# Window stores on POOL's queue, memory's values beside the last scan step, w_co sums behind each cross-attention head

## The chip, the cores and the metric

The kernel runs on one core of a Trainium2 chip. The metric is the device time of one execution in microseconds; a smaller number is better. Matrix products run on PE (TensorE), whose weight loads the profile lists as PEld; elementwise work runs on DVE (VectorE), ACT (ScalarE) and POOL (GpSimd); SP (SyncE) issues nearly all DMAs. Each engine works through its own queue in order.

## The reference, cut to what matters

One layer of a hybrid encoder trunk, on x of 1024 tokens by 1024 channels and a memory of 256 tokens, all in float32:

```python
h = rms_norm(x, g_mix_pre)
aq, ak, av, dqkv, dgate, dalpha, dbeta = split(h @ w_in)
attn_o = window_attention(rope(aq), rope(ak), av, sink)      # 8 heads of 64, 2 key groups, +-128 tokens
dn_o = gated_deltanet(dqkv, dgate, dalpha, dbeta, ...)       # 4 heads of 128, both directions
x = x + rms_norm(concat(attn_o, dn_o) @ w_out, g_mix_post)
q = rms_norm(x, g_cross_pre) @ w_cq                          # 4 heads of 256
k, v = split(rms_norm(mem, g_mem) @ w_ckv)
x = x + rms_norm((softmax(q @ k.T / 16) @ v) @ w_co, g_cross_post)
g, u = split(rms_norm(x, g_ffn_pre) @ w_gate_up)             # 2 x 2816
x = x + rms_norm((silu(g) * u) @ w_down, g_ffn_post)
```

## The kernel before, in words

A float32 product is made of three products of high and low parts. `split` (l.100) casts a tile to its high part on ACT (l.103) and subtracts that from the tile on DVE, or on POOL where `eng` says so (l.104); `load_w` loads a block of weights (`wraw`, l.125) and splits it into `whi` and `wlo`.

The stages follow each other in time as follows, by the times of the profile. Until 355 us: input projection, the preparation of the delta rule and the first windows of attention. From 355 to about 520 us: the scans of the delta rule. Up to 545 us: what is left of the windows and of memory's projection. Then the output projection w_out (`mid_gemm`, PE tile `pmg`), from about 640 us cross-attention, then w_co, the feed-forward's first matrix, and from about 1295 us w_down.

The order in which the stage of the scans is written comes from a table, `ORDER_3` (l.39); `issue` calls one function for each entry. `s01` is one step of the two scans (each has two heads and both directions), interleaved in four pieces; a step loads `kv` and `pz` of the next chunk (l.859, l.860), multiplies them into the PSUM tile `psc` (l.844) and, in the last steps, forms the output `ol`, which PE transposes (l.936) and SP stores (l.941). `W` is `next_windows`: two windows of local attention, of 16 in all (2 groups of 8). `K` is `next_keys`: one block of 128 columns of memory's keys, 24 products of 128x256 into `pck` (l.984). `V` is `next_values`: half of memory's values, 48 products of 128x512 into `pcv` (l.1000). `M` is memory's norm. A scheduler with a model of the engines then arranges the instructions of each engine by their priority, which follows the order of writing. `tc.high_priority(AHEAD)` moves a block forward by 300 places, and `tc.issue_after(ins)` keeps a block behind an instruction.

A window (`window`, l.663) splits the scaled queries into `qs` (ACT, and POOL at l.677), makes four `psw` score tiles (l.685), takes their maxima with `m` (DVE, l.687), exponentials (ACT), scales them by the reciprocal `es` (l.697 to 703; l.703 on DVE for some windows, on ACT for others), transposes them (`ptw`, l.711), splits them to `ph` and `pl` and multiplies with the values into `pow` (l.716). ACT's copy and DVE's addition (l.719, l.720) put the result in `ao`, a tile with one buffer, which is stored to `d_mix` in DRAM. Once all windows and scans of a half of the tokens are there, SP loads `d_mix` back as `mraw` (l.1147) in four quarters, which are split to `s0h` and `s0l` for w_out.

`cross_attention` (l.1182) runs four heads for one half of the tokens, then four for the other: scores `pcs`, softmax `cpr`, its transposes `pct` and their split `cph`, `cpl`, and the products `pco`. Between the two halves stands the code that forms sums of blocks of w_co for a block product with fewer multiplications: four chunks, each with four loads `wpart` and, on DVE, four subtractions (l.1269 to 1274) and four splits. In w_down the PSUM banks `pdX` are added to `za` on DVE (`zv`, l.1775).

The lines of the changed kernel behind l.720 have numbers smaller by one, up to cross-attention.

Of the kernel before, what the change touches and what calls it, by code (L numbers as in the profile page):

```python
# [14 lines left out]
ALU = mybir.AluOpType  # L15
# [8 lines left out]
NT = S // P  # L24
# [4 lines left out]
AHEAD = 300  # L29
# [6 lines left out]

ORDER_1 = ("k0 k1 E0 K0 U0 E1 K1 U1 S0 q0 v0 q1 C0 v1 E2 C1 k2 E3 k3 q2 K2 U2 v2 K3 U3 S1 q3 C2 v3 C3 B0 B1").split()
ORDER_2 = "L0 L1 A4 V A0 A1 G0 G1 L2 L3 W W W A2 A3 G2 G3 W".split()
ORDER_3 = ("M " + "s01 W K " * 5 + "s01 V " + "s01 K " * 2 + "s01 K V").split()


_NAMES = ["ident", "mUi", "mLi", "m5", "m6", "band0", "band1", "band2", "mU", "mL", "ones"]
# [34 lines left out]
def tile_hybrid_block(  # L77
# [6 lines left out]
    nc = tc.nc  # L84
# [15 lines left out]
    def split(hi, lo, src, scale=None, eng=None):  # L100

        if scale is None:
            nc.scalar.copy(hi, src)  # L103
            return (eng or nc.vector).tensor_tensor(lo, src, f32(hi), ALU.subtract)  # L104
        nc.scalar.activation(hi, src, AF.Identity, scale=scale)
        return nc.vector.scalar_tensor_tensor(lo, src, scale, f32(hi), ALU.mult, ALU.subtract)
# [83 lines left out]
    d_mix = dram.tile([D, S], F32, name="d_mix")  # L190
# [28 lines left out]
    pt = small()  # L219
# [3 lines left out]
    for hf in range(2):  # L223
# [12 lines left out]
        for k in range(KT):  # L236
            pt = small()
            for j in range(4):
                nc.tensor.transpose(pt[:, j * P:(j + 1) * P], xts[4 * hf + j][:, k * P:(k + 1) * P], ident)
            g = gcol[:, k:k + 1]  # L240
            cast = nc.scalar.activation(hi[:, k, :], pt, AF.Identity, scale=g)  # L241
            cut = nc.vector.scalar_tensor_tensor(lo[:, k, :], pt, g, f32(hi[:, k, :]), ALU.mult, ALU.subtract)
# [12 lines left out]
    pt = small()  # L255
# [81 lines left out]
    pt = small()  # L337
# [11 lines left out]
    xa, za, ua, ea, la = s64("xa"), s64("za"), s64("ua"), s64("ea"), s64("la")  # L349
# [30 lines left out]
    pt = small()  # L380
# [282 lines left out]
    def window(n, g):  # L663

        tok = slice(n * P, (n + 1) * P)
        k0, k1 = max(n - 1, 0), min(n + 1, NT - 1) + 1
        nb = k1 - k0
        w = nb * P
        band = C[:, _AT["band0"] - C0 + (k0 - n + 1) * P:][:, 0:w]

        khi, klo = (t[:, k0 * P:k1 * P] for t in keys[g])
        qr = tw.tile([P, 4, P], F32, tag="qr", name="qr", bufs=1)
        for r in range(2):
            nc.sync.dma_start(qr[64 * r:64 * r + 64], d_q[256 * g:256 * g + 256, tok].rearrange("(h e) t -> e h t", h=4))
        qs = tw.tile([P, 4, P], F32R, tag="qs", name="qs")
        nc.scalar.copy(qs, qr)
        nc.gpsimd.tensor_tensor(qs[64:128], qr[64:128], f32(qs[64:128]), ALU.subtract)

        m4 = tw.tile([P, 4], F32, tag="m4", name="m4")
        ssum = tw.tile([P, 4], F32, tag="ssum", name="ssum")  # L680
        pr = []
        for hh in range(4):
            pp = pw.tile([P, 512], F32, tag="pw", name="psw")
            for i, kk in enumerate((khi, klo)):
                nc.tensor.matmul(pp[:, 0:w], qs[:, hh, :], kk, start=(i == 0), stop=(i == 1))
            sc = tw.tile([P, 384], F32, tag="sc", name="sc", bufs=8)
            nc.vector.tensor_tensor_reduce(out=sc[:, 0:w], in0=pp[:, 0:w], in1=band, scale=0.125,
                                           scalar=sink[:, 4 * g + hh:4 * g + hh + 1], op0=ALU.add, op1=ALU.max,
                                           accum_out=m4[:, hh:hh + 1])
            pr.append(sc)  # L690
        nm = tw.tile([P, 4], F32, tag="nm", name="nm")
        nc.vector.tensor_scalar(nm, m4, -1.0, None, ALU.mult)
        for hh in range(4):
            nc.scalar.activation(pr[hh][:, 0:w], pr[hh][:, 0:w], AF.Exp, bias=nm[:, hh:hh + 1],
                                 accum_out=ssum[:, hh:hh + 1])
        es = tw.tile([P, 4], F32, tag="es", name="es")
        nc.gpsimd.tensor_tensor(es, sink[:, 4 * g:4 * g + 4], m4, ALU.subtract)
        nc.scalar.activation(es, es, AF.Exp)
        nc.vector.tensor_tensor(es, es, ssum, ALU.add)
        nc.vector.reciprocal(es, es)  # L700
        for hh in range(4):
            if not 7 <= g * NT + n < 13:
                nc.vector.tensor_scalar(pr[hh][:, 0:w], pr[hh][:, 0:w], es[:, hh:hh + 1], None, ALU.mult)
            else:
                nc.scalar.mul(pr[hh][:, 0:w], pr[hh][:, 0:w], es[:, hh:hh + 1])
        yield
        po = pw.tile([P, 4, P], F32, tag="pow", name="pow", bufs=1)
        for j in range(nb):
            pp = pw.tile([P, 512], F32, tag="pw", name="ptw")
            for hh in range(4):  # L710
                nc.tensor.transpose(pp[:, hh * P:(hh + 1) * P], pr[hh][:, j * P:(j + 1) * P], ident)
            ph = tw.tile([P, 512], F32R, tag="ph", name="ph")
            pl = tw.tile([P, 512], F32R, tag="pl", name="pl")
            split(ph, pl, pp)
            for i, pe_ in enumerate((ph, pl)):
                nc.tensor.matmul(po.rearrange("p h t -> p (h t)"), vhl[:, k0 + j, g].rearrange("p r e -> p (r e)"), pe_,
                                 start=(j == 0 and i == 0), stop=(j == nb - 1 and i == 1))
        ao = tw.tile([P, 4, P], F32, tag="ao", name="ao", bufs=1)[0:64]
        nc.scalar.copy(ao, po[64:128])
        nc.vector.tensor_tensor(ao, po[0:64], ao, ALU.add)  # L720
        out_queue = nc.scalar if 5 <= g * NT + n < 8 else nc.sync
        out_queue.dma_start(d_mix[g * 256:(g + 1) * 256, tok].rearrange("(h e) t -> e h t", e=64), ao)

# [456 lines left out]
    def cross_attention(q, hf):  # L1182
        for h in range(4):
# [3 lines left out]
            for tp in range(2):  # L1187
# [11 lines left out]
                for t2_ in range(2):  # L1199
                    n = 2 * tp + t2_  # L1200
# [6 lines left out]
            for kt in range(2):  # L1207
                pt = pn.tile([P, 512], F32, tag="pn", name="pct")
                for t in range(4):
                    nc.tensor.transpose(pt[:, t * P:(t + 1) * P], prs[t // 2][:, t % 2, kt * P:(kt + 1) * P], ident)  # L1210
                ph = tx.tile([P, 512], F32R, tag="cph", name="cph", bufs=2)
                pl = tx.tile([P, 512], F32R, tag="cpl", name="cpl", bufs=2)
                split(ph, pl, pt)
                pts.append((ph, pl))
            for j in range(2):
                po = pn.tile([P, 512], F32, tag="pn", name="pco")
                cs = slice((2 * h + j) * P, (2 * h + j + 1) * P)
                for kt in range(2):
                    for i, (a, b_) in enumerate(((0, 0), (0, 1), (1, 0))):
                        nc.tensor.matmul(po, vr_[a][:, kt, cs], pts[kt][b_], start=(kt == 0 and i == 0),  # L1220
                                         stop=(kt == 1 and i == 2))
                ct = 2 * h + j
                if hf == 0:
                    nc.scalar.copy(raw[:, ct], po)
                    split(q[0][:, ct, :], q[1][:, ct, :], po)
                    continue
                k = ct % HK
                if ct < HK:
                    d_ = s3_raw()[:, k]
                    nc.vector.tensor_tensor(d_, raw[:, k], po, ALU.subtract)  # L1230
                    split(q[0][:, k], q[1][:, k], d_)
                    continue
                split(q[0][:, ct, :], q[1][:, ct, :], po)
                d_ = tx.tile([P, HALF], F32, tag="cs", name="cs")
                nc.vector.tensor_tensor(d_, po, s3_raw()[:, k], ALU.subtract)
                split(*(t[:, k] for t in s2_part()), d_)
                nc.vector.tensor_tensor(raw[:, k], raw[:, k], d_, ALU.add)
                nc.vector.tensor_tensor(raw[:, ct], raw[:, ct], d_, ALU.subtract)

    part, kept = [], []  # L1240

    def s3_raw():
        if not kept:
# [21 lines left out]
    for k in range(HK):  # L1265
        r12, r11, r22, r21 = (wpart(F32) for _ in range(4))
        for t, i, j in ((r12, 0, 1), (r11, 0, 0), (r22, 1, 1), (r21, 1, 0)):
            nc.sync.dma_start(t, w_co[(HK * i + k) * P:(HK * i + k + 1) * P, j * HALF:(j + 1) * HALF])
        nc.vector.tensor_tensor(r11, r12, r11, ALU.subtract)
        nc.vector.tensor_tensor(r12, r22, r12, ALU.subtract)  # L1270
        sum_out(3, k, r12)
        sum_out(1, k, r11)
        nc.vector.tensor_tensor(r22, r22, r11, ALU.subtract)
        nc.vector.tensor_tensor(r21, r21, r22, ALU.subtract)
        sum_out(2, k, r22)
        sum_out(4, k, r21)
# [494 lines left out]
    block_product(D_, "s4", b22, extra=sums)  # L1771
    X = [bank("pdX") for _ in range(4)]
    block_product(X, "s2", b22, last=False, extra=lambda k: sub(b21[:, k], b21[:, k], b22[:, k]))
    for t in range(4):
        nc.vector.tensor_tensor(zv[:, t], za[:, t], X[t], ALU.add)
    late = block_product(X, "s1", b11, first=False)
    for t in range(4):
        nc.vector.tensor_tensor(za[:, t], za[:, t], X[t], ALU.add)
# [94 lines left out]
```

## Time and profile before

| | |
|---|---|
| median of 3 runs | 1513.27 us (1511.99 to 1513.67) |
| profiled execution | 1516.22 us |
| its span | 1514.3 us |
| mean granted PE clock | 0.994 |
| busy PE / PEld / DVE / ACT / POOL | 97 / 82 / 73 / 51 / 24% of the span |
| HBM | 178.63 MB read, 73.70 MB written |

The profile is of one execution. The time of a run is longer than the span because it includes what lies around the first and the last recorded instruction. A row of a timeline gives the start in microseconds, the duration in microseconds, the engine and line, the operation and its tiles; in brackets stands how long the engine was idle before it, and what released it. A row of waits gives the line that waited, what it waited for, the sum in microseconds, how often, and the longest.

### The profile page before, as it was taken

The page shows a single profiled execution, that of the slowest core. Times are in us where ns is not written, and L with a number is a line of the kernel's source. Part 1 is how long each engine was busy: PE and PEld are TensorE (multiplying, and loading weights), DVE is VectorE, ACT ScalarE, POOL GpSimd, SP SyncE. Part 2 cuts the span into 40 slices and gives each one's busy share as a digit, 9 for nine tenths or more (in the row PEclk, how much of TensorE's full clock was granted, in tenths as well). Part 3 has the DMA queues.
Part 4 walks back from the last instruction along what each step waited for, and adds up shares of the span by engine and source line. Part 5 has one row for each costly group of instructions (what it writes and reads, how often), then busy time and mean ns, then how long its engine had stood idle before and what let it go on. Part 6 is the DMA issues. An engine that isn't in the chain of part 4 may idle for free.

```text
span 1514.3 us, 21323 instructions
## 1 busy us (share of the span) xinstructions
PE 1474.7 (97%) x7437; PEld 1240.4 (82%) x7437; DVE 1100.5 (73%) x1801; ACT 778.0 (51%) x1604; POOL 363.0 (24%) x394
## 2 busy tenths in 40 slices
PE   7999999999999999999999999999999999999998
PEld 6888878888898878888788877888888888888787
DVE  5878998577987876538567787776867764696666
ACT  7678844567466764455545674232322232454533
POOL 0011232431225403242201102343534342000030
PEclk9999999999999999999999999999999999999999
DMA  6244555556997584458724654334434433953255
GB/s 203 70 119 135 142 165 138 156 172 168 320 310 244 170 313 154 146 162 264 240 98 166 202 195 125 124 114 132 145 111 142 137 105 107 331 196 98 104 179 169
DMA packets 257751, 256.34 MB, mean 169 GB/s; under 512 B 18128, under 2 KB 190317, under 8 KB 257645
## 3 DMA queue, kind: packets, MB, share of 16 engines
q1 hardware_dynamic: 255677, 252.50, 52.3%
q10 hardware_dynamic: 1968, 2.49, 0.5%
q8 instruction: 58, 0.95, 0.3%
q14 instruction: 48, 0.39, 0.1%
HBM read 178.63 MB, written 73.70 MB: 167 GB/s over the span
## 4 chain that ended last, share of the span: by engine, by line
PE 64%; DVE 11%; DMA 7%; issue 3%; SPq 1%; ACT 1%; POOL 1%; DVEq 0%; ACTq 0%; POOLq 0%
PE pE L1508 8%; PE pD L1508 8%; PE pmg L1105 6%; PE pA L1508 6%; PE pdX L1716 6%; PE pst L1321 5%; PE pB L1508 4%; PE pcq L276 3%; PE psc L844 3%; PE pdA L1716 2%; PE pg L276 2%; PE pdD L1716 2%; DMA wpart<-in_w_co_dram 1%; DMA b<-in_w_down_dram 1%; PE pco L1220 1%
## 5 line engine op out<-in xcount | busy, mean ns | idle before, releaser
L103 ACT CAST whi<-wraw 128x1024 fp32r<-128x1024 f32 x96 | 100.7, 1050 | 120.1 <-DMA wraw<-in_w_gate_up_dram 36.0
L276 PE MATMUL pg<-hlo,whi 128*128 128x512 f32 x352 | 141.0, 401 | 0.0
L276 PE MATMUL pg<-hhi,whi 128*128 128x512 f32 x352 | 140.5, 399 | 0.0
L276 PE MATMUL pg<-hhi,wlo 128*128 128x512 f32 x352 | 140.2, 398 | 0.0
L104 POOL TENSOR_TENSOR wlo<-wraw,whi 128x1024 fp32r<-128x1024 f32 x36 | 87.2, 2424 | 185.1 <-ACT whi L103 184.9
L1508 PE MATMUL pA<-b,whi 128*128 128x512 f32 x352 | 109.8, 393 | 2.0 <-ACT whi L103 1.0
L104 DVE TENSOR_TENSOR wlo<-wraw,whi 128x1024 fp32r<-128x1024 f32 x60 | 74.7, 1245 | 39.6 <-ACT whi L103 35.6
L1508 PEld LDWEIGHTS pA<-b,whi 128*128 128x128 f32 x352 | 65.3, 188 | 17.1 <-ACT whi L103 1.9
L276 PEld LDWEIGHTS pg<-hhi,whi 128*128 128x128 f32 x352 | 67.2, 191 | 13.5 <-ACT hhi L241 0.3
L276 PEld LDWEIGHTS pg<-hhi,wlo 128*128 128x128 f32 x352 | 67.3, 191 | 12.7
L1716 PE MATMUL pdX<-dhl,whi 128*128 128x512 f32 x264 | 76.1, 390 | 1.5 <-ACT dhl L103 0.8
L276 PEld LDWEIGHTS pg<-hlo,whi 128*128 128x128 f32 x352 | 67.1, 191 | 12.7
L1593 POOL TENSOR_TENSOR act<-act,up 128x512 f32<-128x512 f32 x33 | 51.0, 1546 | 82.9 <-DVE up L1592 61.8
L103 ACT CAST whi<-araw 128x1024 fp32r<-128x1024 f32 (+1 forms) x36 | 35.3, 981 | 68.2 <-PE pdX L1716 27.6
L1508 PE MATMUL pA<-b,wlo 128*128 128x512 f32 x176 | 69.0, 392 | 0.5 <-DVE wlo L104 0.5
L104 DVE TENSOR_TENSOR wlo<-araw,whi 128x1024 fp32r<-128x1024 f32 (+1 forms) x36 | 40.8, 1132 | 36.4 <-ACT whi L103 36.3
L1565 POOL TENSOR_TENSOR sr<-wraw 128x512 f32<-128x512 f32 x22 | 30.2, 1371 | 142.2 <-DMA wraw<-in_w_gate_up_dram 98.1
L301 DVE SCALAR_TENSOR_TENSOR acc<-cp,cols,acc 128x1024 f32<-128x1024 f32 x48 | 63.0, 1314 | 0.2
L1716 PEld LDWEIGHTS pdX<-dhl,whi 128*128 128x128 f32 x264 | 49.3, 188 | 12.7 <-ACT dhl L103 1.1
L103 ACT CAST dhl<-b 128x512 fp32r<-128x512 f32 x66 | 40.3, 619 | 31.3 <-PE pdA L1716 13.5
L1508 PE MATMUL pB<-s0h,s1h 128*128 128x512 f32 x176 | 54.3, 390 | 0.5 <-ACT s1h L103 0.5
L1508 PE MATMUL pD<-x,s3h 128*128 128x512 f32 x176 | 54.2, 389 | 0.0
(503 smaller groups left out, 4257.8 us busy)
## 6 DMA issues: line engine op xcount, KB each, us to landing
wraw<-in_w_gate_up_dram SPq DMA_DIRECT2D x54, 512.0 KB, 3.9
kv<-d_kv SPq DMA_DIRECT2D x32, 512.0 KB, 7.5
wraw<-in_w_in_dram SPq DMA_DIRECT2D x22, 512.0 KB, 3.7
b<-in_w_down_dram SPq DMA_DIRECT2D x20, 512.0 KB, 6.5
araw<-d_as SPq DMA_DIRECT2D x20, 512.0 KB, 3.7
pz<-d_pz SPq DMA_DIRECT2D x32, 256.0 KB, 6.0
wraw<-in_w_ckv_dram SPq DMA_DIRECT2D x16, 512.0 KB, 4.7
wraw<-in_w_out_dram SPq DMA_DIRECT2D x16, 512.0 KB, 4.0
```

The costliest lines, as they stand in the source:

```text
L103: nc.scalar.copy(hi, src)
L104: return (eng or nc.vector).tensor_tensor(lo, src, f32(hi), ALU.subtract)
L276: nc.tensor.matmul(p_, w[:, k, :], ah[a][:, k, :], start=(k == 0 and i == 0), stop=(k == nk - 1 and i == 2))
L301: nc.vector.scalar_tensor_tensor(acc, cp[:, t:t + S], taps[t], acc, ALU.mult, ALU.add)
L844: nc.tensor.matmul(out[:, d, h, :], lt[:, d, h, :], rt[:, d, h, :], start=True, stop=True)
L1105: nc.tensor.matmul(pp[t], act[a][:, k, tt], w_[:, kk, :], start=(k == 0 and i == 0), stop=(k == KT - 1 and i == 2))
L1220: nc.tensor.matmul(po, vr_[a][:, kt, cs], pts[kt][b_], start=(kt == 0 and i == 0), stop=(kt == 1 and i == 2))
L1321: nc.tensor.matmul(bank, a[:, tt], w, start=(start and i == 0), stop=(stop and i == 2), skip_group_check=not check)
L1508: nc.tensor.matmul(out_, w[a][:, k, :], xx[b_][:, k, :], start=(start and k == 0 and i == 0), stop=(k == HK - 1 and i == 2), skip_group_ch ...
L1565: nc.gpsimd.tensor_tensor(s[0], b_[:, 0:HK], b_[:, HK:], ALU.add)
L1593: nc.gpsimd.tensor_tensor(o_, o_, up, ALU.mult)
L1716: nc.tensor.matmul(banks[t], a[:, k - k0, tt], w, start=(first and k == 0 and i == 0), stop=(k == NB - 1 and i == 2), skip_group_check=not ...
```

## The change

It has five parts. The store of `ao`, which 13 windows issued from SP and three from ACT, is issued by POOL for all 16. In `ORDER_3` the first half of memory's values (`V`) moves from the sixth step of the scans to a place ahead of the last step, and all key blocks come before it. Window 7's softmax scaling goes from ACT to DVE. The first two subtractions of each w_co chunk are kept behind the last `cpl` of the cross-attention head of the same number. And the four `zv` additions of w_down get a higher priority.

```diff
-ORDER_3 = ("M " + "s01 W K " * 5 + "s01 V " + "s01 K " * 2 + "s01 K V").split()
+ORDER_3 = ("M " + "s01 W K " * 5 + "s01 K " * 3 + "V s01 V").split()
...
-            if not 7 <= g * NT + n < 13:
+            if not 8 <= g * NT + n < 13:
                 nc.vector.tensor_scalar(pr[hh][:, 0:w], pr[hh][:, 0:w], es[:, hh:hh + 1], None, ALU.mult)
...
-        out_queue = nc.scalar if 5 <= g * NT + n < 8 else nc.sync
-        out_queue.dma_start(d_mix[g * 256:(g + 1) * 256, tok].rearrange("(h e) t -> e h t", e=64), ao)
+        nc.gpsimd.dma_start(d_mix[g * 256:(g + 1) * 256, tok].rearrange("(h e) t -> e h t", e=64), ao)
...
-                split(ph, pl, pt)
+                cut = split(ph, pl, pt)
                 pts.append((ph, pl))
+            turned_at.append(cut)
...
-        nc.vector.tensor_tensor(r11, r12, r11, ALU.subtract)
-        nc.vector.tensor_tensor(r12, r22, r12, ALU.subtract)
+        with tc.issue_after(turned_at[k].ins):
+            nc.vector.tensor_tensor(r11, r12, r11, ALU.subtract)
+            nc.vector.tensor_tensor(r12, r22, r12, ALU.subtract)
...
-    for t in range(4):
-        nc.vector.tensor_tensor(zv[:, t], za[:, t], X[t], ALU.add)
+    with tc.high_priority(2 * AHEAD):
+        for t in range(4):
+            nc.vector.tensor_tensor(zv[:, t], za[:, t], X[t], ALU.add)
```

SP's queue at the start of the scans, before (`pz` and `kv` are the scans' chunk, `kraw` the second group's window keys, `wraw` the first block of w_ckv):

```order
L860 DMA pz<-d_pz_108 128x512
L722 DMA d_mix<-ao 64x4x128
L859 DMA kv<-d_kv_104 128x1024 x2
L731 DMA kraw<-d_k 64x1024
L125 DMA wraw<-in_w_ckv_dram 128x8x128
```

The same place on SP after the change:

```order
L859 DMA pz<-d_pz_108 128x512
L858 DMA kv<-d_kv_104 128x1024 x2
L730 DMA kraw<-d_k 64x1024
L125 DMA wraw<-in_w_ckv_dram 128x8x128
L730 DMA kraw<-d_k 64x1024
```

The store of a window no longer stands between the loads. POOL's queue in the second half of the scans, after the change (`wlo` is a key block's low part):

```order
L721 DMA d_mix<-ao 64x4x128
L104 TENSOR_TENSOR wlo<-wraw,whi 128x1024 x2
L721 DMA d_mix<-ao 64x4x128
L697 TENSOR_TENSOR es<-prm,m_4204 128x4
L677 TENSOR_TENSOR qs<-qr,qs 64x512
```

Each window's store stands now among the other steps of POOL, whose own order is otherwise much as before. PE's queue ahead of the output projection, before (from the last window's scores on):

```order
L1000 MATMUL pcv<-wlo,mT_4077 128x512
L716 MATMUL pow<-ph,vhl 128x512
L685 MATMUL psw<-khi,qs 128x256
L685 MATMUL psw<-klo,qs 128x256
L716 MATMUL pow<-pl,vhl 128x512
L685 MATMUL psw<-khi,qs 128x256
L685 MATMUL psw<-klo,qs 128x256
L685 MATMUL psw<-khi,qs 128x256
L685 MATMUL psw<-klo,qs 128x256
L711 MATMUL ptw<-ident,sc 128x128 x8
```

Behind it follow `pow`, `ptw`, twelve `pcv`, `pow`, `ptw` and then the first `pmg`. The last rows ahead of the first `pmg` after the change:

```order
L685 MATMUL psw<-khi,qs 128x256
L685 MATMUL psw<-klo,qs 128x256
L716 MATMUL pow<-pl,vhl 128x512
L685 MATMUL psw<-khi,qs 128x256
L685 MATMUL psw<-klo,qs 128x256
L685 MATMUL psw<-khi,qs 128x256
L685 MATMUL psw<-klo,qs 128x256
L711 MATMUL ptw<-ident,sc 128x128 x4
L1104 MATMUL pmg<-whi,s0h 128x512
```

The values' products that stood behind the last window's scores now lie ahead of them, among the scores of the window before it; the windows' last transposes and products run into the output projection. DVE's queue in cross-attention, before (the first two subtractions of w_co's first chunk are l.1269 and l.1270; `cmx` are the maxima of a head's scores):

```order
L106 SCALAR_TENSOR_TENSOR s0l<-ptn,cols,s0h 128x512 x2
L1269 TENSOR_TENSOR wpart<-wpart 128x512
L1270 TENSOR_TENSOR wpart<-wpart 128x512
L1273 TENSOR_TENSOR wpart<-wpart 128x512
L104 TENSOR_TENSOR wpart<-wpart 128x512
L1274 TENSOR_TENSOR wpart<-wpart 128x512
L1196 TENSOR_REDUCE cmx<-pcs 128x2
```

After the change the same two subtractions are l.1270 and l.1271:

```order
L104 TENSOR_TENSOR cpl<-pct,cph 128x512
L1195 TENSOR_REDUCE cmx<-pcs 128x2
L104 TENSOR_TENSOR cpl<-pct,cph 128x512
L1270 TENSOR_TENSOR wpart<-wpart 128x512
L1196 TENSOR_SCALAR cmx<-cmx 128x2
L1195 TENSOR_REDUCE cmx<-pcs 128x2
L1271 TENSOR_TENSOR wpart<-wpart 128x512
```

They stood ahead of the first heads' softmax and stand now behind the first head's second `cpl`; so do those of the other three chunks behind the heads after it. In w_down no instruction of any engine stands elsewhere than before.

More of the change, by code (lines that the diff above doesn't have):

```diff
@@ L1238, in cross_attention @@
                 nc.vector.tensor_tensor(raw[:, ct], raw[:, ct], d_, ALU.subtract)
-    part, kept = [], []
+    part, kept, turned_at = [], [], []
     def s3_raw():
```

## The prediction

> **What bounds the kernel now.** I read the page's busy times first, then the busy time of each engine by stage, then PE's waits inside the stages where it is not full, and last the rows around each wait.
>
> ```profile
> span 1514.3 us, 21323 instructions
> PE 1474.7 (97%) x7437; PEld 1240.4 (82%) x7437; DVE 1100.5 (73%) x1801; ACT 778.0 (51%) x1604; POOL 363.0 (24%) x394
> ```
>
> PE is the bound: 1514.3 − 1474.7 = 39.6 us is all the idle time that a change of order can win. The profiled execution took 1516.22 us, 1.92 us outside its span and 2.95 us above the median of the runs shown, 1513.27. I make the sum against 1516.22 and carry the difference over to the median. About 0.2%, 3.0 us, is what a measurement of this kernel can tell from no change.
>
> ```profile
> 355.00:400.00 45.00, 40.36 (x272) 35.94 (x271) 35.46 (x87) 27.88 (x61) 9.64 (x11) 0.96 0.90 274
> 400.00:505.00 105.00, 102.93 (x781) 96.95 (x780) 89.03 (x232) 71.49 (x193) 48.18 (x54) 1.00 0.84 266
> 505.00:550.00 45.00, 40.41 (x234) 33.67 (x234) 36.17 (x76) 30.05 (x73) 7.13 (x12) 0.96 0.74 246
> 705.00:735.00 30.00, 27.14 (x140) 21.65 (x139) 23.52 (x45) 18.57 (x45) 5.44 (x4) 1.00 0.70 234
> ```
>
> Columns: stretch, its length, busy PE, weight loads, DVE, ACT, POOL, clock, DMA share, GB/s. The change touches four stretches: the start of the scans (PE idle 45.00 − 40.36 = 4.64 us), the scans (2.07), their end (4.59) and cross-attention (2.86): 14.16 us in all. PE's waits in the first, third and fourth:
>
> ```profile
> PE psc L844 <- issue: 2.2, 1, 2.2
> PE psw L685 <- DVE m L687: 2.8, 2, 1.8
> PE pow L716 <- DVE pl L104: 1.3, 2, 0.8
> PE pct L1210 <- DVE b L104: 1.6, 1, 1.6
> PE pco L1220 <- DVE cpl L104: 1.0, 1, 1.0
> ```
>
> **The stores and the start of the scans.** The first wait reads "issue", that is, nothing the profile names. SP's rows name it:
>
> ```profile
> SPq L722 <- DVE m L687: 10.2, 1, 10.2
> 358.50 0.33 SPq L860 DMA_DIRECT2D pz<-d_pz  x1
> 363.89 0.62 SPq L722 DMA_DIRECT2D d_mix<-ao  x1
> 364.62 1.02 SPq L859 DMA_DIRECT2D kv<-d_kv  x2
> 369.30 0.46 PE L844 MATMUL psc<-kv,pz 128*128 128x128 f32 x2 [2.23 <-issue]
> ```
>
> SP stood at a window's store until 363.89 us; the scans' first `kv` loads are queued behind it and leave at 364.62, and PE's first scan product on `kv` and `pz` starts at 369.30 after 2.23 us idle. With the store on POOL nothing stands between the `pz` load at 358.50 and the `kv` loads, so these can leave some 5 us sooner, more than the 2.23 that PE waits. What is late next is DVE in this stretch (35.46 of 45.00 busy): I take **−2.0** of 2.23.
>
> ```profile
> L722 SPq DMA_DIRECT2D d_mix<-ao x13: 586/601/1104, 324.1 to 556.0; - x13
> L722 ACTq DMA_DIRECT2D d_mix<-ao x3: 582/607/663, 414.9 to 441.4; - x3
> DMA to landing us min/median/max: 2.5/2.8/8.4
> L677 POOL TENSOR_TENSOR qs<-qr,qs 64x512 fp32r<-64x512 f32 x13 | 16.7, 1283 | 42.3 <-ACT qs L676 28.9 <-DVE m L687 7.2 <-ACT es L698 3.7
> ```
>
> The change frees 13 × 0.601 = 7.8 us of SP and 3 × 0.607 = 1.8 us of ACT. Neither bounds a stage, so beyond the scans' start I count 0. On POOL 16 stores are added, each waiting in POOL's queue for DVE's addition into `ao`; the order shows 7 of them directly ahead of a `qs`, `ol` or `ors` step that PE's next scores or transposes need. No row of before shows a DMA issued by POOL. Its price is bounded from below by 0 (POOL is 24% busy, and it idled 42.3 / 13 = 3.3 us ahead of each `qs`), and from above by the longest thing that holds POOL here, a `wlo` of 2.38 us, at all 16: 38 us. The nearest row is the same DMA on SP, 0.60 us, and most of that fits into POOL's idle: I take a third of 7 × 0.60 = 4.2, so **+1.4**. Since `ao` has one buffer, the next window's first write waits for the store to land, 2.8 us in the median; the 16 stores stand (556.0 − 324.1) / 15 = 15.5 us apart in the mean, so that is hidden unless a store leaves over 10 us late.
>
> The Trainium skill, "DMA: Bandwidth & Descriptors", section "Issuing engines are not separate DMA queues", says that another issuing engine saves only the issue time; by that alone the stores would be worth nothing. The 2.23 us row disagrees: what is saved is not the issue but SP's wait in front of it.
>
> **Memory's values beside the last scan step.** The work is the same: 24 `pck` and 48 `pcv` change places.
>
> ```profile
> 519.39 2.87 PE pck L984 x24
> 541.97 2.77 PE pcv L1000 x12
> 515.32 0.50 PE L716 MATMUL pow<-pl,vhl 128*128 128x512 f32 x1 [0.50 <-DVE pl L104]
> 518.13 0.44 PE L685 MATMUL psw<-khi,qs 128*128 128x384 f32 x1 [1.02 <-DVE m L687]
> ```
>
> A key block is 2.87 us of PE and half of the values 48 × 2.77 / 12 = 11.1 us. In the order after, 36 `pcv` (8.3 us) come before the last transposes of the scans' output, where one key block stood, and the bare `psw` pairs of 515 to 518 us get products between them. Of 0.50 + 1.02 = 1.52 us I take **−1.2**. An earlier step has 2.87 us where it had 11.1: two steps with a key block alone run now in a stretch with 2.07 us of idle, so I count 0, and at worst +1 (2.07 / 2). Then the end:
>
> ```profile
> 526.03 9.02 DMA mraw<-d_mix
> 530.51 2.59 DVE L104 TENSOR_TENSOR s0l<-mraw,s0h 128x1024 fp32r<-128x1024 f32 x2 [0.90 <-ACT s0h L103]
> 533.77 0.50 PE L716 MATMUL pow<-ph,vhl 128*128 128x512 f32 x1 [0.22 <-ACT ph L103]
> 535.29 0.50 PE L716 MATMUL pow<-pl,vhl 128*128 128x512 f32 x1 [0.79 <-DVE pl L104]
> 536.15 1.23 DVE L104 TENSOR_TENSOR s0l<-mraw,s0h 128x1024 fp32r<-128x1024 f32 x1 [0.91 <-ACT s0h L103]
> 537.84 0.58 PE L685 MATMUL psw<-khi,qs 128*128 128x256 f32 x1 [1.81 <-DVE m L687]
> ```
>
> PE idles 0.22 + 0.79 + 1.81 = 2.82 us because DVE subtracts four `mraw` quarters (and waits for their landing) ahead of the last window's reductions, while 12 `pcv` that need none of this stand behind, at 541.97. After, no `pcv` is left behind that window, and 60 of them lie between the last scan transposes and the first w_out product. But the last eleven products before w_out are then the window's own, with nothing between, and DVE still subtracts the `mraw` quarters between two windows' reductions; their landing is bound by the scans' last store, which the change hardly moves. So part stays: **−2.0** of 2.82, with bounds +1 (the quarters land as late and hold two windows) and −2.8.
>
> **w_co sums behind each head.**
>
> ```profile
> DVE wpart L1269 <- DMA wpart<-in_w_co_dram: 8.1, 3, 4.3
> 726.47 0.69 DVE L1269 TENSOR_TENSOR wpart<-wpart 128x512 f32<-128x512 f32 x1 [4.31 <-DMA wpart<-in_w_co_dram]
> ```
>
> DVE stands three times, 8.1 us, at a w_co chunk that has not landed, with softmax and splits of the same head behind it. After, a chunk's first two subtractions follow the head's last `cpl`; a late chunk then holds only the next head's work, and has some microseconds more to land. Of PE's 1.6 + 1.0 us I take **−2.2**: DVE is busy 23.52 of 30.00 us, so it can catch up. The sums themselves are needed only in the w_co stage.
>
> **Window 7 and the bank sums.**
>
> ```profile
> 544.24 1.13 DVE L703 TENSOR_SCALAR sc<-sc,es 128x256 f32<-128x256 f32 x4
> 1415.31 2.47 DVE L1775 TENSOR_TENSOR zv<-za,pdX 128x512 f32<-128x512 f32 x4
> 1416.14 0.70 PE L1716 MATMUL pdX<-dhl,whi 128*128 128x512 f32 x2 [0.75 <-DVE zv L1775]
> ```
>
> Window 7 puts four scalings, 1.13 us, on DVE instead of ACT: 0 while PE has scan products to go on with, 1.1 if it has none. The four `zv` additions of w_down get a higher priority, but in the order of DVE and PE they stand where they stood: 0, and the 0.75 us wait stays.
>
> **The sum:** −2.0 − 1.2 − 2.0 − 2.2 = −7.4, plus 1.4, is −6.0: 1516.22 − 6.0 = 1510.2 for a profiled execution, and **1507.3** for the median. By the bounds the gains alone go from −1 to −9.
>
> **The rivals.**
>
> *POOL's stores take the place of the waits (slower).* POOL and DVE hold each other up in this trace:
>
> ```profile
> L1197 DVE TENSOR_SCALAR cmx<-cmx x16: 152/160/1849, 686.6 to 795.2; 128x2 f32<-128x2 f32 x16
> 714.54 2.41 POOL L104 TENSOR_TENSOR wlo<-wraw,whi 128x1024 fp32r<-128x1024 f32 x1 [9.40 <-ACT whi L103]
> 715.12 1.85 DVE L1197 TENSOR_SCALAR cmx<-cmx 128x2 f32<-128x2 f32 x1
> L697 POOL TENSOR_TENSOR es<-prm,m 128x4 f32<-128x4 f32 x15 | 4.0, 266 | 25.9 <-DVE m L687 25.2
> 411.62 1.18 POOL L697 TENSOR_TENSOR es<-prm,m 128x4 f32<-128x4 f32 x1
> ```
>
> A DVE step of 0.16 us took 1.85 beside a POOL `wlo`, and a POOL step of 0.27 took 1.18 beside DVE. A store in POOL's queue waits for DVE's addition, and may then be held in the same way; `es`, `qs` and `wlo` behind it start later, and PE waits for them. It decides from 7.4 / 16 = 0.46 us for each store that reach PE. At the excess of that `es` row, 0.91: 16 × 0.91 = 14.6, less 7.4, is +7.2 and **1520.5**. For it speaks DVE's load in the scans (89.03 of 105.00 us); against it, POOL's idle. The Trainium skill, "SBUF — State Buffer", section "SBUF: two separate sides", speaks for this rival: DVE can lock POOL out of a shared port, and then a DMA issued by POOL waits for its descriptors. The two stretched rows agree that the engines exclude each other; no row here shows it for a DMA. Chance 0.24.
>
> *The gains are swallowed.* In the scans DMA is 0.84 to 0.90 busy and DVE 85%. If `kv` is late whenever it leaves, and the `mraw` quarters hold DVE as now, only cross-attention's −2.2 is left, against +1.4: −0.8, **1512.5**. Chance 0.14.
>
> *More than the named waits.* With SP free all through the scans, and stores that cost nothing, three quarters of the four stretches' idle go: 14.16 × 0.75 = 10.6, **1502.7**. Chance 0.15.
>
> *That the change does not do what it says* holds for the bank sums, which don't move, and is in the sum.
>
> **How the numbers follow.** The forecast, 1507.3, has 0.47. Faster by over 0.2% is it and the larger gain: 0.47 + 0.15 = 0.62; within 0.2%: 0.14; slower: 0.24. The range goes from 1501.0, 1.7 below the larger gain, to 1518.0, where a store costs 0.76 us ((4.7 + 7.4) / 16); beyond that lies half of the slower case (0.12), and below the range some 0.05. Faster and slower cases share the chance; the forecast's own range is 1504 to 1510.
>
> **What would show it.** Right: the `psc` wait at the scans' start gone and `kv` issued within 1 us of the `pz` load; no `pcv` alone between the last window and w_out; no wait of DVE for a w_co chunk that is followed by one of `pct` or `pco`; PE's busy time unchanged at 1474.7 and its idle 33 to 35 us; the `zv` wait still 0.7. Wrong: POOL's `qs` or `es` released by a store, PE waiting on `psw` or `ptw` throughout 400 to 505 us, `ao` copies that wait for `d_mix`, or a PE idle of over 40 us.

## The result

The changed kernel takes 1506.87 us in the median of 17 runs (1501.73 to 1512.62), the kernel before 1513.67 us beside it (17 runs). The ratio is 0.9955, interval 0.9942 to 0.9967: 6.8 us faster, between 5.0 and 8.8. The forecast was 1507.3, 6.0 less than before. The profiled execution after took 1503.54 us, some 3 us under its median, as that of before stood 3 above its own; the two profiles so lie further apart than the medians.

The page of the changed kernel, its span and the busy times:

```profile
span 1501.6 us, 21335 instructions
PE 1468.7 (98%) x7437; PEld 1238.4 (82%) x7437; DVE 1106.9 (74%) x1805; ACT 777.9 (52%) x1600; POOL 374.3 (25%) x410
```

PE's idle time falls from 39.6 to 32.9 us, by 6.7. Its busy time falls too, by 6.0, at the same 7437 products. The stretches, with the columns of before (idle is the length less the PE column, the third from the end is the clock):

```profile
355.00:400.00 45.00, 41.89 (x316) 38.77 (x315) 39.03 (x103) 28.39 (x65) 11.79 (x12) 1.00 0.95 312
400.00:505.00 105.00, 103.26 (x801) 98.14 (x800) 93.06 (x238) 72.58 (x207) 57.30 (x69) 1.00 0.81 245
505.00:550.00 45.00, 41.99 (x194) 33.75 (x192) 32.64 (x57) 29.42 (x48) 1.75 (x4) 0.92 0.81 282
705.00:735.00 30.00, 30.00 (x149) 25.19 (x148) 24.18 (x36) 18.31 (x37) 10.50 (x5) 1.00 0.75 250
```

In the stretch of cross-attention PE has no idle time left. In the three others 3.11, 1.74 and 3.01 us remain, where before 4.64, 2.07 and 4.59 stood. PE's longest waits in the first and the third, and DVE's for w_co in cross-attention:

```profile
PE psw L685 <- DVE m L687: 2.1, 1, 2.1
PE ptw L711 <- DVE m L687: 2.5, 2, 1.5
DVE wpart L1270 <- DMA wpart<-in_w_co_dram: 2.7, 1, 2.7
```

To see where the time went, I take PE's first scan product, the last product of w_out (`pmg`) and the first of w_co (`pst`) in the timelines; three rows of before, then three of after:

```profile
364.19 0.83 PE L844 MATMUL psc<-kv,pz 128*128 128x128 f32 x6
637.76 0.39 PE L1105 MATMUL pmg<-wlo,b 128*128 128x512 f32 x1
762.39 0.40 PE L1321 MATMUL pst<-whi,b 128*128 128x512 f32 x1
```

```profile
360.30 0.83 PE L843 MATMUL psc<-kv,pz 128*128 128x128 f32 x6
628.71 0.39 PE L1104 MATMUL pmg<-wlo,b 128*128 128x512 f32 x1
749.00 0.40 PE L1322 MATMUL pst<-whi,b 128*128 128x512 f32 x1
```

From the first to the second mark it is 273.6 us before and 268.4 after, from the second to the third 124.6 and 120.3. The stage up to the first mark, which the change hardly touches, is 3.9 us shorter in this pair. Two of the runs below, whose edits lie behind this stage, reached the first mark at 360.3 and 361.2 us, so this is scatter between executions. It is most of what the profiles differ by beyond the medians. I call the two lengths **scans to w_out** and **cross** below.

### The profile page after: what moved, and what is told of

Read it like the earlier page. It is cut to its first block, busy times and chain, and to the rows that moved or that the text cites. A ratio compares the mean times of both kernels' runs of the same rounds, so it can differ in the third digit from the quotient of the medians.

```text
span 1501.6 us, 21335 instructions
## 1 busy us (share of the span) xinstructions
PE 1468.7 (98%) x7437; PEld 1238.4 (82%) x7437; DVE 1106.9 (74%) x1805; ACT 777.9 (52%) x1600; POOL 374.3 (25%) x410
## 4 chain that ended last, share of the span: by engine, by line
PE 68%; DVE 6%; DMA 3%; ACT 3%; issue 1%; SPq 0%; POOL 0%; ACTq 0%; DVEq 0%
PE pE L1509 8%; PE pD L1509 8%; PE pcq L276 6%; PE pmg L1104 6%; PE pA L1509 6%; PE pdX L1717 6%; PE pst L1322 5%; PE pB L1509 4%; PE psc L843 3%; PE pdA L1717 2%; PE pdD L1717 2%; PE pg L276 2%; PE pcs L1193 2%; PE pco L1220 1%; PE pck L983 1%
## 5 line engine op out<-in xcount | busy, mean ns | idle before, releaser
L1567 DVE TENSOR_TENSOR sr<-sr,wraw 128x512 f32<-128x512 f32 x22 | 36.6, 1665 | 24.4 <-POOL sr L1566 24.4
```

Source lines behind the costliest of these rows:

```text
L1567: nc.vector.tensor_tensor(s[1], s[0], a_[:, 0:HK], ALU.subtract)
```

## Experiments

Each ran for 12 executions or nearly (the first hold of the tail 7) beside runs of the kernel before. "us" is the ratio to before, less 1, times the time of before.

| kernel | ratio (interval) | us | scans to w_out | cross |
|---|---|---|---|---|
| before | 1 | | 273.6 | 124.6 |
| changed kernel | 0.9955 (0.9942 to 0.9967) | -6.8 | 268.4 | 120.3 |
| stores on POOL alone | 1.0030 (1.0016 to 1.0045) | +4.5 | 277.7 | 125.5 |
| ORDER_3 alone | 0.9993 (0.9978 to 1.0008) | -1.1 | 271.3 | 123.3 |
| w_co subtractions alone | 0.9978 (0.9967 to 0.9989) | -3.3 | 273.8 | 120.3 |
| ORDER_3 + w_co | 0.9982 (0.9969 to 0.9995) | -2.7 | 273.3 | 120.3 |
| ORDER_3 + w_co + window 7 | 0.9998 (0.9985 to 1.0011) | -0.3 | 276.4 | 120.3 |
| POOL + ORDER_3 | 1.0007 (0.9995 to 1.0020) | +1.1 | 270.5 | 123.0 |
| POOL + ORDER_3 + w_co | 0.9990 (0.9978 to 1.0002) | -1.5 | 273.4 | 120.3 |
| changed, tail held | 0.9957 (0.9943 to 0.9971) | -6.5 | 270.6 | 120.3 |
| changed, low parts in pieces | 0.9988 (0.9973 to 1.0002) | -1.8 | 278.2 | 120.3 |
| pieces, stores on SP and ACT | 0.9965 (0.9948 to 0.9982) | -5.3 | 271.0 | 120.3 |
| pieces, window 7 on ACT | 1.0006 (0.9988 to 1.0023) | +0.9 | 280.0 | 120.3 |
| pieces, tail held | 1.0008 (0.9990 to 1.0025) | +1.2 | 282.9 | 120.3 |

The two last columns are of one profiled execution each; the changed kernel and the one with its tail held, level in time, lie 2.2 us apart in them. Every row made from the changed kernel has the higher priority of the bank sums too.

**Stores on POOL alone.**

```diff
-        out_queue = nc.scalar if 5 <= g * NT + n < 8 else nc.sync
-        out_queue.dma_start(d_mix[...], ao)
+        nc.gpsimd.dma_start(d_mix[...], ao)
```

> The kernel before with one edit: all 16 window stores on POOL. By the prediction's terms: the wait of 2.23 us at the scans' start goes (-2.0), the stores cost POOL +1.4, in all -0.6 us. By the reading of the two traces (PE's clock is 0.50 to 0.75 from 371 to 375 us of before, behind that wait, and 1.00 there after) the half pace goes too: -2.2 and some -1.7, so -3 to -4 us, with kv issued within 1 us of the last pz load and no clock under 0.95 from 365 to 380 us. By the rival (stores on POOL hold qs, es and ol): +5 to +12 us, with PE waiting for psw or ptw between 400 and 505 us.

It is 4.5 us slower (2.4 to 6.8), a little under the range that the rival gave. But the rival's mechanism is not what its trace shows. PE's longest waits from 400 to 560 us:

```profile
PE pow L716 <- ACT ph L103: 2.8, 3, 1.3
PE psw L685 <- DVE m L687: 1.7, 2, 1.0
PE ptw L711 <- DVE m L687: 1.6, 1, 1.6
PE psc L843 <- DVE kv L871: 1.2, 3, 0.6
```

None of PE's waits there is for POOL, and the wait at the scans' start is gone as foretold. The clock, though, doesn't stay up as expected: it is 0.68 and 0.50 from 377 to 381 us, behind another wait. There DVE's scalings meet a key block's low part on POOL and take 3.52 us (1.41 for such a four in the scans without it), and the reductions for PE's next scores stand behind them:

```profile
371.61 3.52 DVE L703 TENSOR_SCALAR sc<-sc,es 128x384 f32<-128x384 f32 x4
371.78 2.47 POOL L104 TENSOR_TENSOR wlo<-wraw,whi 128x1024 fp32r<-128x1024 f32 x1 [5.54 <-ACT whi L103]
376.31 0.44 PE L685 MATMUL psw<-khi,qs 128*128 128x384 f32 x1 [2.16 <-DVE m L687]
```

This wait, of 2.14 to 2.16 us, stands in all five kernels with the stores on POOL and whole low parts, the changed kernel among them; in those with stores on SP and ACT no `psw` wait of this stretch is over 0.4 us. So the earlier loads exchange one wait of some 2 us for another.

The rest of the loss lies behind: PE idles 3.5 us from 400 to 505 us and 6.8 from there to 560, where before it was 2.1 and 4.6. The scheduler, given another place for the stores, has also arranged PE, DVE and ACT otherwise there. That this arrangement costs the time is argued, not shown.

**ORDER_3 alone.**

```diff
-ORDER_3 = ("M " + "s01 W K " * 5 + "s01 V " + "s01 K " * 2 + "s01 K V").split()
+ORDER_3 = ("M " + "s01 W K " * 5 + "s01 K " * 3 + "V s01 V").split()
```

> The kernel before with one edit: ORDER_3 of the change. By the prediction: -1.2 (last scan step) and -2.0 (tail), -3.2 us. By the rival that the landing of the mraw quarters holds two windows' reductions in either order: the waits move from psw at 537.8 us to ptw some 13 us behind the last transposes of ol, the clock halves behind them as before, and the sum is -1 to +1 us. The wait at the scans' start (2.2 us, then half pace) stays in both.

-1.1 us (-3.3 to +1.2): told neither from zero nor from the forecast of 3.2 less. Its trace speaks for the rival in part. In the tail PE waits 2.5 us at `psw`, 1.6 at `pcv` and 0.9 at `pmg`, where before it was 2.8 at `psw` and 1.3 at `pow`. The `psw` wait didn't move to `ptw`, as the rival had it, but it stands behind three `mraw` quarters on DVE, as before:

```profile
528.93 3.68 DVE L104 TENSOR_TENSOR s0l<-mraw,s0h 128x1024 fp32r<-128x1024 f32 x3 [0.26 <-ACT s0h L103]
533.07 0.39 PE L685 MATMUL psw<-khi,qs 128*128 128x256 f32 x1 [2.47 <-DVE m L687]
```

**w_co subtractions alone.**

```diff
+            turned_at.append(cut)
...
+        with tc.issue_after(turned_at[k].ins):
```

> The kernel before with one edit: the first two subtractions of each w_co chunk kept behind a head's last cpl. By the prediction -2.2 us. By the traces of before and after, whose PE rows lie 9.1 us apart where the scores of cross-attention begin and 13.4 where w_co begins: -4.3 us, since waits shorter than those listed go as well. By the rival that the whole gain came from elsewhere: 0. PE idle in the 70 us from the first pct on under 0.5 us by the first two.

-3.3 us (-5.0 to -1.7), and 120.3 us of cross, as in every kernel with this edit; without it cross took 123.0 to 125.5. The stretch from 690 to 765 us of this run:

```profile
690.00:765.00 75.00, 75.00 (x399) 64.31 (x398) 55.76 (x92) 41.05 (x90) 15.17 (x6) 1.00 0.75 254
```

PE never idles there. This is the one part whose gain stands by itself.

**The changed kernel without stores on POOL.**

```diff
-        nc.gpsimd.dma_start(d_mix[...], ao)
+        out_queue = nc.scalar if 5 <= g * NT + n < 8 else nc.sync
+        out_queue.dma_start(d_mix[...], ao)
```

> The changed kernel with the stores back on SP (13) and ACT (3). By the prediction the stores on POOL were worth 0.6 us, so this is 0.6 slower than the changed kernel and 5.4 faster than before. By the reading of the clock they were worth 3 to 4 us: -3 to -4 against before, with the 2.2 us wait of psc and the half pace back at the scans' start. By the rival (POOL's stores cost) this is faster than the changed kernel: -9 us or more against before.

All but the stores give -0.3 us, 6.5 short of the changed kernel. The stores, which cost 4.5 us on the kernel before, are worth 6.5 here, so the parts don't add up. The 2.0 us wait at the scans' start is back, with half pace behind it. In the tail PE waits 3.8 us for DVE's reductions (2.7 in ORDER_3 + w_co), and a wait of 2.7 us stands in the scans; the rows of DVE, of POOL and of PE's waits:

```profile
414.82 5.02 DVE L703 TENSOR_SCALAR sc<-sc,es 128x256 f32<-128x256 f32 x4
414.44 4.73 POOL L104 TENSOR_TENSOR wlo<-wraw,whi 128x1024 fp32r<-128x1024 f32 x2 [2.74 <-PE pck L984]
PE psc L844 <- DVE kv L872: 2.7, 1, 2.7
```

and the same two places in the changed kernel:

```profile
413.07 1.14 DVE L703 TENSOR_SCALAR sc<-sc,es 128x256 f32<-128x256 f32 x4
415.43 2.39 POOL L104 TENSOR_TENSOR wlo<-wraw,whi 128x1024 fp32r<-128x1024 f32 x1 [5.20 <-ACT whi L103]
```

These are window 7's scalings, which the change moved to DVE. Beside two key blocks' low parts on POOL they take 5.02 us, and ahead of them 1.14. In ORDER_3 + w_co, with these scalings on ACT, no `psc` wait in the scans is over 0.4 us.

**Window 7 back on ACT, with and without stores on POOL; POOL and ORDER_3.**

```diff
-            if not 8 <= g * NT + n < 13:
+            if not 7 <= g * NT + n < 13:
```

> The changed kernel with window 7's four scalings back on ACT. By the prediction (window 7 costs 0, at most 1.1 us): within 1 us of the changed kernel, -6 to -7 us against before. By the theory that the stores on POOL move the scan's work out of the way of key blocks' low parts on POOL, so that DVE's scalings (1.14 us for four in the changed kernel, 5.02 in the run without stores on POOL) run free: also the same. By the rival that window 7 on DVE is what makes the stores on POOL pay: slower than the changed kernel by 4 us or more.

> The changed kernel without its stores on POOL and without window 7's move: ORDER_3 and the w_co subtractions alone. Sum of their single runs: -0.5 to -1 and -3.3, so -4 us. By the theory that window 7 on DVE cost the run without stores on POOL its gain (four scalings of 5.02 us beside two wlo on POOL, PE waiting 2.7 us at kv): -4 to -5 us, and 3.5 to 4.5 faster than that run, without a psc wait over 1 us between 400 and 430 us. By the rival (that run was slow by its tail, a psw wait of 3.8 us): -0.5 us as there.

> The kernel before with two edits: stores on POOL and ORDER_3. If the parts add up: +4.6 - 0.7, so +4 us. By the theory that the stores on POOL as such cost nothing and that their single run was slow because the scheduler arranged the scans and the tail otherwise: the scans' start gains 3.4 us (wait and half pace), the scans and tail lose what the order costs without them, in all -3 to -4 us. By the rival that a store on POOL costs some tenths of a microsecond wherever it stands: +2 to +5 us.

With stores on POOL, window 7's move is worth -6.8 + 1.5 = -5.3 us (their intervals together some 2.6 either way); without them it costs 2.4 (2.8 either way), not told from zero. The rival won in the first case; in the second the gain of 3.5 to 4.5 us that I expected from taking the move out is not shown, and ORDER_3 + w_co stays at -2.7 where I expected -4 to -5. The stores themselves, on ORDER_3 and w_co without window 7, are worth +1.2 us (2.7 either way), and on ORDER_3 alone +2.2 (3.0 either way): not the gain of 3 to 4 that I expected. POOL + ORDER_3, at +1.1 (-0.8 to +3.0), fits neither the -3 to -4 nor clearly the rival's +2 to +5. In the trace with window 7 on ACT, DVE, POOL and PE in the scans:

```profile
446.25 2.70 DVE L692 TENSOR_SCALAR nm<-m 128x4 f32<-128x4 f32 x1
446.56 2.35 POOL L104 TENSOR_TENSOR wlo<-wraw,whi 128x1024 fp32r<-128x1024 f32 x1
449.59 0.80 PE L716 MATMUL pow<-pl,vhl 128*128 128x512 f32 x1 [2.07 <-DVE pl L104]
```

Here a later window meets a low part: a step on four numbers for each partition takes 2.70 us, the split behind it is late, PE waits 2.07 us and takes the next products at half pace (0.80 us for a `pow` of 0.39). In the changed kernel the same low part meets nothing on which PE waits that long. One collision of 2.1 us and the half pace behind it are shown. From 505 to 560 us PE idles another 2.1 us more than in the changed kernel; what that has to do with window 7, and what makes up the rest of 5.3 us, is not shown.

**Low parts in pieces.** This tests the collision itself: four POOL instructions of 128x256 in place of one of 128x1024.

```diff
+                for i in range(0, k, k // pieces):
+                    ks = slice(i, i + k // pieces)
+                    eng.tensor_tensor(lo[:, ks], raw[:, ks], f32(hi[:, ks]), ALU.subtract)
```

> The changed kernel with one more edit: a key block's low part is formed on POOL in four instructions of 128x256 instead of one of 128x1024. Theory: a POOL instruction holds up a DVE instruction of one kind (scalings and other steps with a scalar operand: nm of 0.17 us took 2.70, four scalings of 1.13 us took 5.02) for its whole length, 2.4 us, and where PE waits for that it loses 2 us and then runs at half pace; pieces of 0.6 us hold it for 0.6. Then the psw wait of 2.1 us at 372 us of the changed kernel falls under 0.8, and the time is -2 to -4 us against the changed kernel. Rival: these waits come from DVE's load, not from POOL: 0, or slower by some tenths of a microsecond for each of the 24 added instructions.

> The run before (key blocks' low parts in pieces) with the window stores back on SP and ACT. Theory: with the long holds gone the stores on POOL are worth what the scans' start shows, the wait of 2.0 us and the half pace behind it, so this is 3 to 4 us slower than with the stores on POOL, not 6.5 us as without pieces; no DVE scaling over 1.2 us. Rival (a store on POOL has a price of its own, and window 7's move hid it): equal or faster.

> Pieces, stores on POOL, and window 7's scalings back on ACT. Theory: window 7's move was worth 5 us on top of the stores on POOL and cost 2.4 without them only by what met a long low part; with pieces it is worth within 1.5 us of nothing. Rival (ACT is too full for window 7's scalings): 4 to 5 us slower than with them on DVE, as without pieces.

All rows of the scaling on DVE (minimum, median, maximum), in the changed kernel, then with pieces, with stores on POOL and without:

```profile
L703 DVE TENSOR_SCALAR sc<-sc,es x44: 347/414/2533, 294.7 to 539.7; 128x384 f32<-128x384 f32 x32, 128x256 f32<-128x256 f32 x12
```

```profile
L709 DVE TENSOR_SCALAR sc<-sc,es x44: 347/416/900, 297.6 to 551.1; 128x384 f32<-128x384 f32 x32, 128x256 f32<-128x256 f32 x12
```

```profile
L709 DVE TENSOR_SCALAR sc<-sc,es x44: 348/414/933, 297.5 to 546.3; 128x384 f32<-128x384 f32 x32, 128x256 f32<-128x256 f32 x12
```

The longest scaling falls from 2.53 to 0.90 us. In all four kernels with pieces it is 0.90 to 0.93; in the ten with whole low parts it is 2.5 to 2.6 in seven, and 0.6 in the three where no scaling starts during one. With stores on POOL the `psw` wait of 2.1 us near 372 us is gone as well; with stores on SP and ACT it wasn't there before either. That a POOL instruction holds these steps of DVE for up to about its own length, and that the `psw` wait came from this, is so shown. Without stores on POOL the pieces bring -5.3 us where there was -0.3, a gain of 5.0 (3.2 either way). With them they bring nothing: 5 us slower than the changed kernel, not the 2 to 4 faster that I expected. Beside the changed kernel PE idles 2.0 us less from 355 to 400 us, where the collision was, but 1.8 more from there to 505 and 4.3 more up to 560. The tail's longest wait:

```profile
536.03 0.79 PE L722 MATMUL pow<-ph,vhl 128*128 128x512 f32 x1 [4.51 <-ACT ph L103]
```

A window's `ph` stands on ACT behind the casts of the `mraw` quarters. So the expectation on the stores fell: with pieces they cost 3.5 us (3.4 either way) instead of bringing 3 to 4. And window 7's move measures -2.7 us with pieces, 3.4 either way, which leaves open whether the collisions were all of its worth.

**The tail held.** Twice, at another place the second time and with pieces:

```diff
+            with tc.issue_after(maxima[2 * NT - 2].ins):       # first: behind window 14's negated maxima
+            with tc.issue_after(cuts[2 * NT - 3, 1].ins):      # second: behind window 13's second split
                 split(mxT[hf][0][:, k2, :], mxT[hf][1][:, k2, :], raw[:, k2, :])
```

> The changed kernel with one more edit: the splits of the mraw quarters kept behind the negated maxima of window 14, so that DVE's reductions of that window, which free the PSUM banks that ptw waits for, no longer stand behind a quarter that has not landed. By the theory: PE's waits of 1.46 and 1.02 us at 521 and 523 us go, and with them the half pace from 523 to 530 us (3.4 us): -3 to -6 us against the changed kernel, -10 to -13 against before. By the rival that the quarters' landing sets the first w_out product anyway: 0, with the wait moved to pmg.

> Pieces, and the low parts of the mraw quarters kept on DVE behind the second split of window 13, so that neither the reductions of window 14 nor that split stand behind a quarter that has not landed. Theory: PE's waits of some 2.5 us ahead of the output projection, and the half pace of 5 to 7 us behind them (2.5 to 3.5 us lost), go: -3 to -6 us against the run with pieces alone. Rival (as in the first try at the tail, where the wait moved to ph): ACT's casts of the quarters hold ph, or pmg waits for the last quarter: 0 to -1 us.

The first is level with the changed kernel (0.9957 and 0.9955), not 3 to 6 us faster. The waits of `ptw` went, and one longer wait took their place:

```profile
527.39 0.79 PE L716 MATMUL pow<-ph,vhl 128*128 128x512 f32 x1 [4.18 <-ACT ph L103]
```

The hold kept the low parts on DVE back, but not the casts on ACT, where `ph` stands behind two quarters and a window's exponentials. The second, in the arrangement that pieces give, is no faster than that arrangement (+1.2 us against -1.8); PE waits 5.1 us for `ph` there. No version beat the changed kernel.

## Why the prediction came out right, and which steps did not

The sum, -6.0, lies beside the measured -6.8 (-8.8 to -5.0). Its terms did not all hold; they erred both ways and the errors cancel, so the closeness is in good part luck. The step that all idle time, 39.6 us, is all that a change of order can win did not hold either: PE's busy time fell too, by 6.0 us, in part because less of it ran at half pace.

**The scans' start, -2.0: the wait named rightly, what comes behind it not.** SP after:

```profile
355.11 0.33 SPq L859 DMA_DIRECT2D pz<-d_pz  x1
355.49 0.90 SPq L858 DMA_DIRECT2D kv<-d_kv  x2
```

`kv` leaves 0.38 us behind the last `pz` load, and no wait for the loads is listed there (the longest of `psc` is 0.5 us, for DVE). The term counted only the idle time. Before, the clock fell behind the wait (third column from the end):

```profile
369.00:371.00 2.00, 1.70 (x12) 1.70 (x13) 0.47 (x1) 1.99 (x7) 0.00 (x0) 0.89 1.01 253
371.00:373.00 2.00, 1.99 (x9) 1.60 (x8) 0.94 (x2) 1.20 (x5) 0.00 (x0) 0.50 1.21 280
373.00:375.00 2.00, 2.00 (x12) 1.75 (x11) 0.80 (x4) 0.69 (x2) 0.00 (x0) 0.75 1.04 231
```

That is 2 x (0.11 + 0.50 + 0.25) = 1.7 us beside the 2.2 of idle time: 3.9 that the old wait cost. Against it stands what DVE makes late next, which the prediction put at 0.2 us: the `psw` wait of 2.14 us behind the meeting of scalings and low part. The idle time of the stretch fell by 4.64 - 3.11 = 1.5 us, and with the 1.7 of half pace, which did not come back in this execution, the start gained 3.2. With the stores alone on POOL it came back. The line on what would prove the prediction right, that PE's busy time stays at 1474.7, failed for the same reason among others.

**Stores on POOL, +1.4: the price lies elsewhere.** The direct price is low, as taken:

```profile
L721 POOL DMA_DIRECT2D d_mix<-ao x16 | 10.9, 680 | 58.0 <-DVE ao L720 49.1 <-ACT mT L105 4.8 <-ACT qs L676 3.4
DMA to landing us min/median/max: 2.5/5.1/7.2
```

0.68 us on POOL for each, with 58 us of idle time ahead of the 16, and a landing of 5.1 us in the median against 2.8 from SP and ACT, which no `ao` had to wait for long. The Trainium skill ("SBUF — State Buffer", "SBUF: two separate sides") speaks of a DMA that takes five times as long when a DVE copy keeps POOL from writing its descriptors. No store here is near that; POOL's rows go from 0.63 to 0.87 us, and the median landing is 1.8 times that of SP and ACT:

```profile
L721 POOL DMA_DIRECT2D d_mix<-ao x16: 633/650/872, 320.9 to 559.1; - x16
```

What the term lacked is that the earlier loads and the stores on POOL change what meets what behind them: the `psw` wait, and, as far as the traces tell, another arrangement of scans and tail. On the old order the store's edit cost 4.5 us with the start's gain already in it, and on ORDER_3 and w_co +1.2, within the noise.

**The last scan step and the tail, -1.2 and -2.0: not shown.** ORDER_3 alone is -1.1 (-3.3 to +1.2). In the changed kernel PE's idle time from 505 to 550 us fell by 1.6, but its clock fell from 0.96 to 0.92, some 1.8 us of these 45. The step that failed is that the `pcv` placed between the windows' scores would cover the `mraw` quarters. DVE's rows and PE's in the tail after:

```profile
519.84 1.23 DVE L104 TENSOR_TENSOR s0l<-mraw,s0h 128x1024 fp32r<-128x1024 f32 x1 [1.58 <-ACT s0h L103]
520.98 0.61 DVE L687 CUSTOM_DVE_ANT_0 sc<-psw,C,prm 128x384 f32<-128x384 f32 x1
521.66 0.66 PE L711 MATMUL ptw<-ident,sc 128*128 128x128 f32 x4 [1.46 <-DVE m L687]
```

DVE stands at a quarter that has not landed, the reduction behind it is late, and the transposes, whose PSUM tiles come from the same pool as the scores, wait for it. The prediction named this as what stays ("they hold two windows") and gave it too little weight. The half pace follows, here for 7 us:

```profile
523.00:525.00 2.00, 1.54 (x5) 1.04 (x5) 1.97 (x5) 1.98 (x7) 0.19 (x1) 0.55 1.03 410
525.00:527.00 2.00, 1.71 (x6) 1.35 (x6) 0.90 (x4) 2.00 (x7) 0.00 (x0) 0.50 1.02 406
527.00:529.00 2.00, 2.00 (x6) 1.39 (x6) 2.00 (x6) 2.00 (x3) 0.00 (x0) 0.50 1.03 407
529.00:531.00 2.00, 2.00 (x8) 1.62 (x7) 2.00 (x3) 0.02 (x1) 0.00 (x0) 0.74 0.66 212
```

**w_co behind the heads, -2.2: right, if anything too small.** -3.3 (-5.0 to -1.7) measured alone, 4.3 between the marks; the term counted two listed waits of 2.6 us, and all 2.86 us of the stretch's idle time went.

**Window 7, 0: the step that failed most.** It is worth -5.3 us with stores on POOL. The prediction asked only how long the scalings take on DVE and what PE has to do meanwhile, not what of POOL's they meet, although it quoted the rows that show POOL and DVE holding each other up, and used them for the stores alone. How much of the 5.3 is such meetings stays open.

**Bank sums, 0: right.** The wait is still there:

```profile
PE pdX L1717 <- DVE zv L1777: 0.7, 1, 0.7
```

So the terms as the runs give them, each on top of those before it, are: ORDER_3 and w_co -2.7, stores on POOL +1.2, window 7 -5.3, in all -6.8. The forecast had nearly the same total from -5.4, -0.6 and 0.

## What to carry to other kernels

Where a scheduler arranges the queues, the parts of a change don't add up: measure an edit on the order it will live in, and read single gains only where a stage is closed off, as cross-attention was here. Of a step that is moved to DVE, ask which long POOL instructions run at that time, and the other way round; cutting POOL's instructions in pieces bounds what they hold, though here the time fell by it only where the stores were on SP and ACT. Price a stall of PE with what follows it: the clock's rows behind the wait belong to its cost.

## What the runs showed of the hardware

- The clock's price of a stall. At the scans' start a spell of half pace cost 1.7 us by the clock's rows in each of seven kernels (1.72 before), and twice that, 3.4, in the changed kernel without stores on POOL; in the tail after it was 3.4 too. A wait of PE is followed by half pace, but not always. Behind 2.23 us of idle time at 369 us (before) and 1.46 and 1.02 us at 522 us (after) the granted clock went to 0.50 for 4 to 7 us. The `psw` wait of 2.14 to 2.16 us that five kernels have was followed by 0.50 in two of them (stores alone, tail held) and by 1.00 in three; what decides is not shown. After the change it stayed at 1.00:

```profile
374.35 0.44 PE L685 MATMUL psw<-khi,qs 128*128 128x384 f32 x1 [2.14 <-DVE m L687]
375.00:377.00 2.00, 2.00 (x20) 2.00 (x18) 1.30 (x4) 1.25 (x4) 1.22 (x2) 1.00 1.05 407
```

- A POOL subtraction of 128x1024 holds a DVE step with a scalar operand for up to its length: 2.70 us instead of 0.17 for one, 5.02 instead of 1.14 for four beside two of them, and 0.90 to 0.93 at most for one scaling where POOL's instruction was cut in four. The Trainium skill ("SBUF — State Buffer", "Who interferes with whom") says that steps of this kind on DVE can contend with POOL, and that whichever comes first then shuts the other out for its whole instruction; the rows of DVE agree.
- A store issued by POOL took 0.65 us of POOL and landed in 5.1 us, one issued by SP or ACT 0.60 us and 2.8 us (medians), for the same 128 KB in 256 pieces.
